# An mLSTM memory layer with its key transposes and one head's output transpose taken from TensorE to VectorE and DRAM

## The chip, the cores and the metric

One core of a Trainium2 chip runs the whole program. The metric is the device time of one execution in microseconds (us); the kernel before takes 935.12 us, the median of 3 runs (934.95 to 935.29). One further execution was profiled, and all durations and starting times below come from it.

## The reference, cut to what matters

The program is one inference step of a two-layer decoder: 256 prompt tokens and 64 sample tokens (8 sequences of 8) share the weights. Layer 0 mixes tokens by chunked spatial gating, layer 1 by an mLSTM matrix memory with 8 heads (keys of 128, values of 256), and each layer ends in a gated feed-forward part. The change lies in layer 1, the memory layer:

```
def step(carry, inp):
    C, n, m = carry
    qc, kc, vc, ic, fc = inp
    ...
    sc = jnp.einsum('bhtd,bhsd->bhts', qc, kc) * w_intra
    num = w_inter[..., None] * jnp.einsum('bhtd,bhde->bhte', qc, C) \
        + jnp.einsum('bhts,bhse->bhte', sc, vc)
    ...
    h = num / jnp.maximum(jnp.abs(den), jnp.exp(-m_t))[..., None]
    ...
    kg = kc * g[..., None]
    decay = jnp.exp(bL + m - m_new)
    C_new = decay[..., None, None] * C + jnp.einsum('bhsd,bhse->bhde', kg, vc)
```

After it each head's `h` is normalised over its 256 values, multiplied by a gate of `o`, and goes through the output projection. So a head needs its keys in two orders: key dimension on the partitions for the scores `sc`, and token on the partitions for `kg` (the new state contracts over tokens). And its normalised rows come out with the token on the partitions, while the output projection wants the value dimension there.

## The kernel before, in words

Weights stream from memory in chunks of 128 x 1024 numbers (`raw`). Products are made of three matmuls of split numbers: ScalarE rounds a chunk to `wh` (`CAST wh`, L181), VectorE makes the rest `wl = raw - wh` (L182), and TensorE does `xh wh`, `xl wh`, `xh wl` for each of the 8 slices, 24 matmuls a block into a PSUM tile `pm`. Four `raw` buffers are filled by SyncE, which waits in its queue until a buffer is free; there are three pairs `wh`, `wl`, so a chunk can be split only when the chunk three before it has been used up. The split of the next chunk is issued ahead of the current block.

The memory layer goes through the heads in pairs (`first_of` for the even head, `second_of` for the odd one). For a head: block q and block k (projections; L934 to L948 add the convolution and give `qs`, once for q and once for k); for an even head the values of both heads (`pv`, `pvs`); then

- `scores`: `psc` = key-query products on TensorE; VectorE makes `Pf` (L1057) from it, `weigh` splits it into `Ph`, `Pl` and makes `Ps`;
- `k_nat`: TensorE turns the keys by three transposes into the PSUM tile `pk` (`turn`): two for the 256 prompt keys, one for the sample keys. ScalarE and VectorE then make `kz` (sample keys with their gates, two halves: ScalarE L1090, VectorE L1091) and `kgh`, `kgl` (gated prompt keys, split, two halves each: L1095, L1096);
- an o block (`o_b`, L1208, then `th_o`);
- `hand_over`: `inter` (8 small matmuls of the old state, `num<-C,Qz`) and `state_sample` (16 matmuls `pcs`, first with the first half of `kz`, then with the second), then VectorE adds `pcs` to the decayed state `C` (L1136);
- `close`, after the following block: 11 matmuls `num`, and `state_prompt`: 6 matmuls `pCp` of `kgh`, `kgl` and the values, which ScalarE copies out (`Cp`, L1203);
- `stats`: the normalised rows `hn` on ScalarE (L1178), which need `nb` on VectorE (L1176) and `sl` on GpSimd. In the heads named in `OFF`, VectorE then turns `hn` in 32x32 blocks (`tb`, L1181), SyncE writes the tile to DRAM (`turn`) and reads it back in four pieces with the blocks exchanged (`hT`, in `back`), and `finish` multiplies it by the gate (`y_b`, six pieces, L1196) and splits the result (`yhb` L1230, `ylb` L1231). In the other heads (0 and 7) `finish` lets TensorE turn `hn` by six transposes into PSUM (`phn`, L53 and L57), and `y_b` (L1228) reads that. `finish(0)` stands inside the second o block of head 1, between its 5th and 6th slice.

Instructions of an engine run in one queue in the order in which they are written, rearranged ahead of time by a scheduler under `behind(...)`, which puts work after a named instruction. PSUM has 3 tiles for `pm`, `pk` and `pvs` and 5 for all else (`psc`, `num`, `pcs`, `pCp`, `pv`, `phn`).

Of the kernel before, what the change touches and what calls it, by code (L numbers as in the profile page):

```python
# [10 lines left out]
F32 = mybir.dt.float32  # L11
F32R = mybir.dt.float32r
# [28 lines left out]
class Net:  # L41
# [745 lines left out]
    def layer_b(self):  # L787
# [5 lines left out]
        with ExitStack() as ctx:  # L793
# [225 lines left out]
            def turn(h):  # L1019
                s = S[h]  # L1020
                ks = s["k"][0]
                s["pk"] = pk = self.psm.tile([P, 512], F32, tag="pm", name="pk")
                for t in range(3):
                    self.tr(pk[:, t * P:(t + 1) * P], ks[:, t * P:(t + 1) * P] if t < 2 else s["ks"], self.ident)

            def scores(h):
# [46 lines left out]
                                               mk[:, NB:NB + 1], Pr.bitcast(F32).rearrange("p (g s) -> p g s", g=4),  # L1073
                                               op0=MULT, op1=ADD)

            def k_nat(h):
                s = S[h]
                if h:
                    turn(h)
                pk = s["pk"]  # L1080
# [5 lines left out]
                kz = hp.tile([P, 2, P], F32R, tag="kz", name="kz", bufs=1)  # L1086
                src = pk[:, 2 * P:3 * P]

                for i in range(2):
                    nc.scalar.activation(kz[:, i, :], src, AF.Copy, scale=gm[:, i, h:h + 1])  # L1090
                    s["kz"] = nc.vector.scalar_tensor_tensor(kz[:, i, :], src, gm[:, 2 + i, h:h + 1], kz[:, i, :].bitcast(F32), op0=MULT, op1=ADD)  # L1091
                for t in range(2):
                    g = colsT[:, t, 32 + h:33 + h]
                    src = pk[:, t * P:(t + 1) * P]
                    nc.scalar.activation(kgh[:, t, :], src, AF.Copy, scale=g)  # L1095
                    nc.vector.scalar_tensor_tensor(kgl[:, t, :], src, g, kgh[:, t, :].bitcast(F32), op0=MULT, op1=SUB)  # L1096
                s["kg"] = (kgh, kgl, kz)
# [32 lines left out]
            def state_out(h, g):  # L1130
                s = S[h]
                dec, C0, pcs = s["P"][2], s["C"][g], s["pcs"][g]
                for u in range(2):
                    b = 2 * g + u
                    s["decayed"] = nc.scalar.activation(C0[:, u, :DV], C0[:, u, :DV], AF.Copy, scale=dec[:, b:b + 1])
                nc.vector.tensor_tensor(C0[:, :, :DV], C0[:, :, :DV], pcs.rearrange("p (u v) -> p u v", u=2), op=ADD)  # L1136
# [76 lines left out]
            def finish(h):  # L1213
                s = S[h]
                yh = hp.tile([P, 2, T], F32R, tag="yhb", name="yhb", bufs=6)
                yl = hp.tile([P, 2, T], F32R, tag="ylb", name="ylb", bufs=6)
                for e in range(2):
                    if h not in OFF:
                        pt = self.psa.tile([P, 512], F32, tag="pa", name="phn")
                        for t in range(2):  # L1220
                            self.tr(pt[:, t * P:(t + 1) * P], hn[:, t, e * P:(e + 1) * P], self.ident)
                        self.tr_some(pt[:, TP:384].rearrange("p (d g s) -> p d g s", d=2, g=4), hn[:, 2, e * P:(e + 1) * P],
                                     self.ident.rearrange("p (g d s) -> p d g s", g=4, d=2))
                    y = self.tp.tile([P, T], F32, tag="yf", name="y_b", bufs=2)
                    if h in OFF:
                        turned_y(h, e, y)
                    else:
                        nc.vector.scalar_tensor_tensor(y, s["o"][e], 1.0, pt[:, :T], op0=ADD, op1=MULT)  # L1228
                    g = gnh[:, 2 * h + e:2 * h + e + 1]
                    nc.scalar.activation(yh[:, e, :], y, AF.Copy, scale=g)  # L1230
# [25 lines left out]
            def blk():  # L1256
                return self.block(KD, self.x_rhs)
# [22 lines left out]

            def first_of(p):
                h = 2 * p
                ps = blk()
                close(h - 1)
                qk_epi(h, 0, ps)
                if h - 2 in OFF:
                    with self.behind(S[h - 1]["sent"]):
                        back(h - 2)
                ps = blk()
                qk_epi(h, 1, ps)  # L1290
                if h - 2 in OFF:
# [12 lines left out]
                v_out(p)  # L1304
                ps = blk()
                o_epi(h, 0, ps)
                hand_over(h)

            def second_of(p):
                h = 2 * p + 1  # L1310
                if p == 0:
                    with self.behind(chosen):
                        self.prefetch(0, self.used + 2)
                ps = blk()
                if p == 0:
# [12 lines left out]
                qk_epi(h, 1, ps)  # L1328
                if h - 2 in OFF:
                    with self.behind(S[h]["halves"][1]):  # L1330
                        finish(h - 2)
                state_in(h)
                ps = blk()
                o_epi(h - 1, 1, ps)
                stats(h - 1)
                if h < NH - 1:
                    rows_in(h + 1)
                if h < NH - 1:
                    ps = blk()
                    o_epi(h, 0, ps)  # L1340
                else:
                    for m in (4, 5):
                        out(m)
                scores(h)
                weigh(h)
                k_nat(h)
                if h == NH - 1:
                    for m in (6, 7):
                        out(m)
                if h == NH - 1:  # L1350
                    with self.behind(S[h - 1]["sent"]):
                        back(h - 1)
                    with self.behind(self.last_sum):
                        finish(h - 1)
                if h < NH - 1:
                    if p:
                        ps = blk()
                    else:
                        ps = self.psm.tile([P, 512], F32, tag="pm", name="pm")
                        (wh, wl), _ = self.take()  # L1360
                        self.rows(ps, wh, wl, 5, self.x_rhs, True, False)
                        finish(0)
                        self.rows(ps, wh[:, 5:, :], wl[:, 5:, :], 3, lambda k: self.x_rhs(5 + k), False, True)
# [4 lines left out]
                    hand_over(h)  # L1368

            scores(0)  # L1370
            k_nat(0)
            with self.behind(S[0]["kz"]):
                weigh(0)
            for p in range(NH // 2):
# [191 lines left out]
```

## Time and profile before

| | |
|---|---|
| median of the runs | 935.12 us |
| the profiled execution's own time | 935.03 us |
| its span from first to last instruction | 933.2 us |
| TensorE matmul (PE) busy | 926.8 us, 99% |
| VectorE (DVE) busy | 689.4 us, 74% |
| ScalarE (ACT) busy | 507.6 us, 54% |
| granted TensorE clock | 1.00 |
| the memory layer lies at about | 418 to 694 us |

A row of the timeline gives start, duration, engine, line, operation with its output and inputs, and in brackets how long the engine stood idle before it and what ended that. PE rows are matmuls, PEld rows the loading of their stationary operand; the ends of PE rows are modelled and overlap, so distances between starts of PEld rows tell more. Durations on the other engines include a part that overlaps the next instruction as well, so the distance of two starts (the pitch) is what an instruction takes in a full queue. In a row of the windows view each engine's busy time is followed by the number of its instructions, then come the granted clock, the share of DMA time and GB/s.

### The profile page before, as it was taken

The page shows a single profiled execution, that of the slowest core. Times are in us where ns is not written, and L with a number is a line of the kernel's source. Part 1 is how long each engine was busy: PE and PEld are TensorE (multiplying, and loading weights), DVE is VectorE, ACT ScalarE, POOL GpSimd, SP SyncE. Part 2 cuts the span into 40 slices and gives each one's busy share as a digit, 9 for nine tenths or more (in the row PEclk, how much of TensorE's full clock was granted, in tenths as well). Part 3 has the DMA queues.
Part 4 walks back from the last instruction along what each step waited for, and adds up shares of the span by engine and source line. Part 5 has one row for each costly group of instructions (what it writes and reads, how often), then busy time and mean ns, then how long its engine had stood idle before and what let it go on. Part 6 is the DMA issues. An engine that isn't in the chain of part 4 may idle for free.

```text
span 933.2 us, 16783 instructions
## 1 busy us (share of the span) xinstructions
PE 926.8 (99%) x6301; PEld 896.7 (96%) x6301; DVE 689.4 (74%) x1283; ACT 507.6 (54%) x892; POOL 110.9 (12%) x312
## 2 busy tenths in 40 slices
PE   9999999999999999999999999999999999999997
PEld 8889999999999999998989989989999999999997
DVE  6768985597777764458998999798788777775541
ACT  7558544455454543346777776575646454553341
POOL 2410000010000001013221112001003111100001
PEclk9999999999999999999999999999999999999999
DMA  8865444455455455457776878675475454455622
GB/s 290 239 192 170 136 139 157 144 151 153 144 156 146 148 155 146 145 166 231 212 239 202 256 228 252 196 240 172 149 222 155 143 156 145 149 152 152 202 68 69
DMA packets 64001, 162.62 MB, mean 174 GB/s; under 512 B 8608, under 2 KB 24744, under 8 KB 63920
## 3 DMA queue, kind: packets, MB, share of 16 engines
q1 hardware_dynamic: 63568, 160.56, 56.4%
q8 instruction: 50, 0.82, 0.4%
q0 software_dynamic: 208, 0.73, 0.2%
q14 instruction: 31, 0.25, 0.1%
q10 hardware_dynamic: 144, 0.26, 0.1%
HBM read 147.20 MB, written 14.32 MB: 173 GB/s over the span
## 4 chain that ended last, share of the span: by engine, by line
PE 96%; DVE 2%; DMA 0%; POOL 0%; issue 0%; ACT 0%; SPq 0%; DVEq 0%; ACTq 0%; POOLq 0%
PE pm L50 76%; PE pv L50 9%; PE pvs L50 3%; PE num L50 2%; PE pyt L50 1%; PE pmix L50 1%; PE py L50 1%; PE pCp L50 1%; PE pcs L50 1%; PE psc L50 0%; DMA raw<-in_a_wv 0%; DVE bcv L942 0%; DVE wl L182 0%; PE pk L53 0%; PE pyt L53 0%
## 5 line engine op out<-in xcount | busy, mean ns | idle before, releaser
L181 ACT CAST wh<-raw 128x1024 fp32r<-128x1024 f32 (+4 forms) x252 | 254.7, 1012 | 279.8 <-PE pm L50 143.4
L182 DVE TENSOR_TENSOR wl<-raw,wh 128x1024 fp32r<-128x1024 f32 (+4 forms) x252 | 299.1, 1187 | 111.9 <-ACT wh L181 109.4
L50 PE MATMUL pm<-xh,wh 128*128 128x320 f32 x1088 | 338.4, 311 | 0.0
L50 PE MATMUL pm<-xh,wl 128*128 128x320 f32 x1088 | 336.2, 309 | 0.0
L50 PE MATMUL pm<-xl,wh 128*128 128x320 f32 x1088 | 336.1, 309 | 0.0
L50 PEld LDWEIGHTS pm<-xh,wh 128*128 128x128 f32 x1088 | 204.3, 188 | 1.7 <-ACT wh L181 0.5
L50 PEld LDWEIGHTS pm<-xl,wh 128*128 128x128 f32 x1088 | 204.3, 188 | 0.2
L50 PEld LDWEIGHTS pm<-xh,wl 128*128 128x128 f32 x1088 | 204.2, 188 | 0.0
L50 PE MATMUL pm<-yh_f,wh 128*128 128x320 f32 x308 | 95.4, 310 | 0.0
L50 PE MATMUL pm<-yl_f,wh 128*128 128x320 f32 x308 | 95.1, 309 | 0.0
L50 PE MATMUL pm<-yh_f,wl 128*128 128x320 f32 x308 | 95.1, 309 | 0.0
L50 PEld LDWEIGHTS pm<-yl_f,wh 128*128 128x128 f32 x308 | 57.9, 188 | 0.0
L50 PEld LDWEIGHTS pm<-yh_f,wh 128*128 128x128 f32 x308 | 57.9, 188 | 0.0
L50 PEld LDWEIGHTS pm<-yh_f,wl 128*128 128x128 f32 x308 | 57.9, 188 | 0.0
L607 DVE SCALAR_TENSOR_TENSOR fcv<-fpad,vecs,fcv 128x336 f32<-128x336 f32 x88 | 49.7, 564 | 1.5
L50 PE MATMUL pv<-wh,xh 128*128 128x512 f32 (+1 forms) x132 | 50.3, 386 | 0.3 <-ACT wh L181 0.3
L50 PE MATMUL pv<-wl,xh 128*128 128x512 f32 (+1 forms) x132 | 50.1, 385 | 0.0
L50 PE MATMUL pv<-wh,xl 128*128 128x512 f32 (+1 forms) x132 | 50.0, 384 | 0.0
L347 DVE TENSOR_TENSOR xT<-pm,xT 128x320 f32<-128x320 f32 x38 | 18.5, 489 | 31.5 <-PE pm L50 31.5
L50 PE MATMUL pm<-yhb,wh 128*128 128x320 f32 x128 | 39.6, 310 | 0.0
L50 PE MATMUL pm<-yh_a,wh 128*128 128x320 f32 x128 | 39.6, 309 | 0.0
L50 PE MATMUL pm<-yl_a,wh 128*128 128x320 f32 x128 | 39.5, 309 | 0.0
(347 smaller groups left out, 1447.6 us busy)
## 6 DMA issues: line engine op xcount, KB each, us to landing
raw<-in_f_up SPq DMA_DIRECT2D x88, 512.0 KB, 3.6
raw<-in_b_win SPq DMA_DIRECT2D x32, 512.0 KB, 4.2
raw<-in_f_dn SPq DMA_DIRECT2D x28, 448.0 KB, 3.4
C<-in_C SPq DMA_DIRECT2D x32, 258.0 KB, 4.6
raw<-in_a_win SPq DMA_DIRECT2D x16, 512.0 KB, 3.7
raw<-in_a_wo SPq DMA_DIRECT2D x16, 512.0 KB, 3.6
raw<-in_b_wv SPq DMA_DIRECT2D x16, 512.0 KB, 3.5
out_Cs<-C SPq DMA_DIRECT2D x32, 256.0 KB, 3.4
```

The lines of the kernel that those rows point to most:

```text
L50: self.pin(self.nc.tensor.matmul(out, lhsT, rhs, start=start, stop=stop))
L181: self.last_split = nc.scalar.copy(wh[:, c, :], raw[:, c, :])
L182: self.last_low = nc.vector.tensor_tensor(wl[:, c, :], raw[:, c, :], wh[:, c, :].bitcast(F32), op=SUB)
L347: self.last_sum = self.nc.vector.tensor_tensor(x, ps[:, :T], x, op=ADD)
L607: nc.vector.scalar_tensor_tensor(cv, pd[:, i:i + NC], self.vec(w + i * KF), cv, op0=MULT, op1=ADD)
```

## The change

`OFF` gets head 0 as well: its `hn` is now turned by VectorE over DRAM, and `finish(0)` moves from the middle of head 1's second o block to the place in head 2 where the other heads have theirs. Its `y_b` is made by six VectorE instructions instead of two.

The prompt keys of heads 1 to 7 are no longer turned by TensorE: `turn` has one transpose left in these heads, the sample keys'. A new `k_turned`, called after block k, lets VectorE turn the 256 prompt keys in 32x32 blocks (`kb`, 128 x 256), writes them to DRAM (`kturn`), and reads them back in four pieces (`kn`, pieces of 64 numbers). `k_nat` is cut in two: `k_sample` makes `kz`, and `k_prompt` makes `kgh`, `kgl` from `kn`, later: behind the values' `vh`, `vl` in even heads, behind the state's decay and sum in odd heads, behind `finish(6)`'s `yh`, `yl` in head 7.

`state_prompt` of the odd heads moves from `close` to behind block k of the following head, so that its six matmuls stand directly in front of the values' `pv`.

```
-OFF = (1, 2, 3, 4, 5, 6)
+OFF = (0, 1, 2, 3, 4, 5, 6)
...
-                for t in range(3):
+                for t in range(2 if h else 0, 3):
                     self.tr(pk[:, t * P:(t + 1) * P], ...
...
+            def k_turned(h):
+                blocks = hp.tile([P, 4, 2, 32], F32, tag="kb", name="kb", bufs=1)
+                nc.vector.transpose(blocks.rearrange("p g t c -> p t g c"),
+                                    S[h]["k"][0][:, :TP].rearrange("p (t g q) -> p t g q", t=2, g=4))
+                nc.sync.dma_start(I["kturn"][h], blocks.rearrange("p g t c -> p (g t c)"))
+                S[h]["kn"] = kn = hp.tile([P, 4, 2, 32], F32, tag="kb", name="kn", bufs=1)
+                for g in range(4):
+                    nc.sync.dma_start(kn[32 * g:32 * g + 32].rearrange("p j t c -> p j (t c)"),
+                                      I["kturn"][h].rearrange("(j q) (g x) -> g q j x", j=4, g=4)[g])
...
-            def k_nat(h):
+            def k_sample(h):
...
+            def k_prompt(h):
...
+                    src = s["kn"][:, :, t, :] if h else s["pk"][:, t * P:(t + 1) * P].rearrange("p (j c) -> p j c", j=4)
+                    nc.scalar.activation(hi, src, AF.Copy, scale=g)
+                    nc.vector.scalar_tensor_tensor(lo, src, g, hi.bitcast(F32), op0=MULT, op1=SUB)
...
             def close(h):
...
-                if h < NH - 2:
+                if h % 2 == 0 and h < NH - 2:
                     state_prompt(h)
...
             def first_of(p):
...
                 ps = blk()
+                state_prompt(h - 1)
                 qk_epi(h, 1, ps)
+                k_turned(h)
...
-                k_nat(h)
+                k_sample(h)
                 values(p, 3)
                 v_out(p)
+                with self.behind(S[h]["vh"], S[h]["vl"]):
+                    k_prompt(h)
...
             def second_of(p):
...
                 qk_epi(h, 1, ps)
+                k_turned(h)
...
-                k_nat(h)
+                k_sample(h)
...
-                    if p:
-                        ps = blk()
-                    else:
...
-                        finish(0)
...
-                    o_epi(h, 1, ps)
+                    o_epi(h, 1, blk())
...
                     hand_over(h)
+                    with self.behind(S[h]["decayed"], S[h]["added"]):
+                        k_prompt(h)
```

The scheduler's order of VectorE in head 1, from the `Pf` of its scores to the second half of `kz`, which the second half of `pcs` needs. Before:

```order
L1057 SCALAR_TENSOR_TENSOR Pf<-psc,w 128x448
L182 TENSOR_TENSOR wl<-raw,wh 128x1024
L1042 SCALAR_TENSOR_TENSOR w<-mb,cols,mxb 128x64
L361 TENSOR_TENSOR Pl<-Pf,Ph 128x384
L1072 SCALAR_TENSOR_TENSOR Ps<-Pf,mk,Pr 128x4x16
L1091 SCALAR_TENSOR_TENSOR kz<-pk,gm,kz 128x128
L1228 SCALAR_TENSOR_TENSOR y_b<-th_o,phn 128x320 x2
L1091 SCALAR_TENSOR_TENSOR kz<-pk,gm,kz 128x128
```

The same stretch of VectorE's queue with the change:

```order
L1057 SCALAR_TENSOR_TENSOR Pf<-psc,w 128x448
L182 TENSOR_TENSOR wl<-raw,wh 128x1024
L1195 STREAM_TRANSPOSE tb<-hn 128x6x4x32
L361 TENSOR_TENSOR Pl<-Pf,Ph 128x384
L1072 SCALAR_TENSOR_TENSOR Ps<-Pf,mk,Pr 128x4x16
L1095 SCALAR_TENSOR_TENSOR kz<-pk,gm,kz 128x128
L1222 TENSOR_TENSOR o_b<-pm,rb 128x320
L1042 SCALAR_TENSOR_TENSOR w<-mb,cols,mxb 128x64
L182 TENSOR_TENSOR wl<-raw,wh 128x1024
L1095 SCALAR_TENSOR_TENSOR kz<-pk,gm,kz 128x128
```

The second `kz` has moved behind head 0's transpose, an `o_b` and the split of a further weight chunk; the two `y_b` that stood ahead of it are gone. Both of its halves still come from the PSUM tile `pk`.

The same stretch of VectorE's queue in head 3, before, from `Pf` on:

```order
L1057 SCALAR_TENSOR_TENSOR Pf<-psc,w 128x448
L1091 SCALAR_TENSOR_TENSOR kz<-pk,gm,kz 128x128
L182 TENSOR_TENSOR wl<-raw,wh 128x1024
L361 TENSOR_TENSOR Pl<-Pf,Ph 128x384
L1072 SCALAR_TENSOR_TENSOR Ps<-Pf,mk,Pr 128x4x16
L1091 SCALAR_TENSOR_TENSOR kz<-pk,gm,kz 128x128
L1208 TENSOR_TENSOR o_b<-pm,rb 128x320
L182 TENSOR_TENSOR wl<-raw,wh 128x1024
```

And with the change:

```order
L1057 SCALAR_TENSOR_TENSOR Pf<-psc,w 128x448
L1245 SCALAR_TENSOR_TENSOR ylb<-y_b,gnh,yhb 128x320 x2
L182 TENSOR_TENSOR wl<-raw,wh 128x1024
L1195 STREAM_TRANSPOSE tb<-hn 128x6x4x32
L361 TENSOR_TENSOR Pl<-Pf,Ph 128x384
L1072 SCALAR_TENSOR_TENSOR Ps<-Pf,mk,Pr 128x4x16
L1095 SCALAR_TENSOR_TENSOR kz<-pk,gm,kz 128x128
L1222 TENSOR_TENSOR o_b<-pm,rb 128x320
L182 TENSOR_TENSOR wl<-raw,wh 128x1024
L1095 SCALAR_TENSOR_TENSOR kz<-pk,gm,kz 128x128
```

Here `ylb` and `tb` stood in front of `Pf` before, so that these only changed sides; what is new in front of the second `kz` is the `o_b` and the second `wl`, which followed it before. The order in head 5 changes in the same way, but there four blocks of the output projection stand between the scores and `pcs`.

The last place is TensorE where the values of head 2 begin, with the change (`pv_5504` and `pv_5505` are the PSUM tiles of the two prompt halves; the words in brackets name the engine whose semaphore the matmul waits for):

```order
L50 MATMUL pCp_5443<-vl_4510,kgh_5330 128x258
L50 MATMUL pCp_5443<-vh_4509,kgl_5331 128x258
L50 MATMUL pv_5504<-wh_5415,xh_77 128x512 [waits DVE_49]
L50 MATMUL pv_5504<-wh_5415,xl_78 128x512
L50 MATMUL pv_5504<-wl_5416,xh_77 128x512
L50 MATMUL pv_5505<-wh_5415,xh_77 128x512 [waits Activation_49]
L50 MATMUL pv_5505<-wh_5415,xl_78 128x512
```

Before, block k with its 24 matmuls stood between the last `pCp` and the first `pv`. Three of the five PSUM tiles hold head 1's `num` until `hn` is made, the fourth is `pCp`, the fifth the first `pv`; the second `pv` gets the tile of `pCp`, once ScalarE has copied it out. In ScalarE's queue that copy (`Cp`) stood ahead of a `CAST wh` and of q's `CAST qh` before, and stands directly behind these two now; heads 4 and 6 have the same order on both engines.

More of the change, by code (lines that the diff above doesn't have):

```diff
@@ L1079, in k_nat @@
                     turn(h)
-                pk = s["pk"]
+                kz = hp.tile([P, 2, P], F32R, tag="kz", name="kz", bufs=1)
+                src = s["pk"][:, 2 * P:3 * P]
+                for i in range(2):
+                    nc.scalar.activation(kz[:, i, :], src, AF.Copy, scale=gm[:, i, h:h + 1])
+                    s["kz"] = nc.vector.scalar_tensor_tensor(kz[:, i, :], src, gm[:, 2 + i, h:h + 1], kz[:, i, :].bitcast(F32), op0=MULT, op1=ADD)
+                s["kg"] = (None, None, kz)
+            def k_prompt(h):
+                s = S[h]
                 if h < NH - 2:
@@ L1085, in k_nat @@
                     kgh, kgl = self.late_keys(h)
[L1086 to L1091, printed above, removed]
                 for t in range(2):
                     g = colsT[:, t, 32 + h:33 + h]
[L1094 to L1097, printed above, removed]
+                    src = s["kn"][:, :, t, :] if h else s["pk"][:, t * P:(t + 1) * P].rearrange("p (j c) -> p j c", j=4)
+                    hi, lo = [x[:, t, :].rearrange("p (j c) -> p j c", j=4) for x in (kgh, kgl)]
+                    nc.scalar.activation(hi, src, AF.Copy, scale=g)
+                    nc.vector.scalar_tensor_tensor(lo, src, g, hi.bitcast(F32), op0=MULT, op1=SUB)
+                s["kg"] = (kgh, kgl, s["kg"][2])
             def rows_in(h):
@@ L1135, in state_out @@
                     s["decayed"] = nc.scalar.activation(C0[:, u, :DV], C0[:, u, :DV], AF.Copy, scale=dec[:, b:b + 1])
-                nc.vector.tensor_tensor(C0[:, :, :DV], C0[:, :, :DV], pcs.rearrange("p (u v) -> p u v", u=2), op=ADD)
+                s["added"] = nc.vector.tensor_tensor(C0[:, :, :DV], C0[:, :, :DV], pcs.rearrange("p (u v) -> p u v", u=2), op=ADD)
                 s["sent"] = nc.sync.dma_start(O["Cs"][h, :, 2 * g:2 * g + 2, :], C0[:, :, :DV])
@@ L1354, in second_of @@
                         finish(h - 1)
+                    with self.behind(S[h - 1]["yh"], S[h - 1]["yl"]):
+                        k_prompt(h)
                 if h < NH - 1:
-                    if p:
-                        ps = blk()
-                    else:
-                        ps = self.psm.tile([P, 512], F32, tag="pm", name="pm")
-                        (wh, wl), _ = self.take()
-                        self.rows(ps, wh, wl, 5, self.x_rhs, True, False)
-                        finish(0)
-                        self.rows(ps, wh[:, 5:, :], wl[:, 5:, :], 3, lambda k: self.x_rhs(5 + k), False, True)
-                    o_epi(h, 1, ps)
+                    o_epi(h, 1, blk())
                     if p == 2:
@@ L1548 @@
     O = {k: nc.dram_tensor("out_" + k, s, F32, kind="ExternalOutput").ap() for k, s in _OUTS.items()}
-    for k, v in dict(rows=(8, 456), sums=(1, 11 * P), turn=(NH, P, 3 * DV)).items():
+    for k, v in dict(rows=(8, 456), sums=(1, 11 * P), turn=(NH, P, 3 * DV), kturn=(NH, P, TP)).items():
         I[k] = nc.dram_tensor(k, v, F32, kind="Internal").ap()
```

6 lines of the change are left out of this document (4 added, 2 removed).

## Prediction

> **What bounds the kernel now.** I read the page's totals first, then the chain of waits, the windows of the memory layer, the waits of PEld, and last the timelines of the engines around the places that the change touches.
>
> ```profile
> PE 926.8 (99%) x6301; PEld 896.7 (96%) x6301; DVE 689.4 (74%) x1283; ACT 507.6 (54%) x892; POOL 110.9 (12%) x312
> PE 96%; DVE 2%; DMA 0%; POOL 0%; issue 0%; ACT 0%; SPq 0%; DVEq 0%; ACTq 0%; POOLq 0%
> 446.00:473.00 27.00, 26.90 (x226) 24.63 (x228) 25.49 (x66) 20.94 (x53) 7.93 (x19) 1.00 0.72 226
> 473.00:525.00 52.00, 52.00 (x370) 48.00 (x370) 47.85 (x109) 37.78 (x83) 8.60 (x19) 1.00 0.73 230
> 525.00:578.00 53.00, 53.00 (x376) 48.84 (x367) 50.25 (x119) 39.18 (x86) 8.39 (x23) 1.00 0.80 243
> PEld pcs L50 <- DVE kz L1091: 0.8, 2, 0.4
> PEld pw L50 <- issue: 0.8, 1, 0.8
> ```
>
> TensorE sets the time: 99% busy, 96% of the chain. So a matmul taken away is worth its time, and a new wait of TensorE costs its whole length. VectorE's 74% is a mean; in the three windows of heads 1 to 5 it is busy 25.49 of 27, 47.85 of 52 and 50.25 of 53 us, 92 to 95%. Moving work from TensorE to VectorE here puts it on an engine that has 5 to 8% left, and TensorE does wait for it already: for `kz`, in front of `pcs`.
>
> **What TensorE loses.** The loads in head 1, at the key transposes and at the first head's output transposes:
>
> ```profile
> 466.68 0.26 PEld L53 LDWEIGHTS pk<-ident,qs 128*128 128x128 f32 x2
> 466.91 0.14 PEld L53 LDWEIGHTS pk<-ident,ks 128*128 128x128 f32 x1
> 467.02 0.19 PEld L50 LDWEIGHTS pm<-xh,wh 128*128 128x128 f32 x1
> ...
> 469.18 0.30 PEld L53 LDWEIGHTS phn<-ident,hn 128*128 128x128 f32 x2
> 469.80 0.14 PEld L57 LDWEIGHTS phn<-ident,hn 128*128 128x128 f32 x1 [0.32 <-ACT hn L1178]
> ...
> 470.19 0.19 PEld L50 LDWEIGHTS pm<-xh,wh 128*128 128x128 f32 x1
> ```
>
> Three key transposes take 467.02 - 466.68 = 0.34 us, 0.115 each. Two go in each of seven heads: 14 x 0.115 = 1.6 us. Head 0's six `phn` take 470.19 - 469.18 = 1.0 us, with the 0.32 that they wait for `hn`. Together 2.6 us off the bound engine; were everything else free, the profiled execution of 935.03 would come to 932.4. All else in this sum is a wait.
>
> [...]
>
> **What VectorE gets, and the second half of kz in head 1.** VectorE in head 1, and the group of the existing block transposes:
>
> ```profile
> 465.31 0.27 DVE L361 TENSOR_TENSOR khl<-qs,kh 128x128 fp32r<-128x128 f32 x1
> ...
> 468.08 0.16 DVE L1176 SCALAR_TENSOR_TENSOR nb<-mv,sl 128x3 f32<-128x3 f32 x1 [0.75 <-POOL sl L1167]
> ...
> 468.56 0.61 DVE L1057 SCALAR_TENSOR_TENSOR Pf<-psc,w 128x448 f32<-128x448 f32 x1
> 469.10 1.21 DVE L182 TENSOR_TENSOR wl<-raw,wh 128x1024 fp32r<-128x1024 f32 x1
> ...
> 471.21 0.34 DVE L1091 SCALAR_TENSOR_TENSOR kz<-pk,gm,kz 128x128 fp32r<-128x128 f32 x1
> 471.48 0.87 DVE L1228 SCALAR_TENSOR_TENSOR y_b<-th_o,phn 128x320 f32<-128x320 f32 x2
> 472.27 0.34 DVE L1091 SCALAR_TENSOR_TENSOR kz<-pk,gm,kz 128x128 fp32r<-128x128 f32 x1
> ```
>
> ```profile
> L1181 DVE STREAM_TRANSPOSE tb<-hn 128x768 f32<-128x768 f32 x6 | 5.8, 968 | 1.3 <-ACT hn L1178 1.3
> ```
>
> A new `kb` has 256 of `tb`'s 768 columns: 968 x 256/768 = 0.32 us, an estimate. From the queue's order in head 1, what lands ahead of the second `kz` is `kb` 0.32, `tb` 0.9 (0.97 less its overlap), an `o_b` 0.40 and a weight split 1.13 (pitches from the rows of head 3 below); the two `y_b` in front of it go, 472.27 - 471.48 = 0.79. Sum: 1.96 us. It ends at 472.27 + 0.34 + 1.96 = 474.57. Who waits:
>
> ```profile
> 472.72 0.19 PEld L50 LDWEIGHTS pcs<-vh,kz 32*128 32x128 f32 x4 [0.41 <-DVE kz L1091]
> ...
> 472.95 0.20 PEld L50 LDWEIGHTS pcs<-vh,kz 32*128 32x128 f32 x4
> ```
>
> The second half of `pcs` loads at 472.95. With the transposes gone TensorE is 0.23 + 1.0 us earlier, ready at 471.7; it gets `kz` at 474.6 (0.05 from VectorE's end to the load, as in head 3). A wait of 2.9 us. Behind it in TensorE's queue stands all that follows, first the next o block. VectorE's queue is full here but for 0.75 us in which `nb` waits for `sl`; that pause doesn't absorb `kb`, since GpSimd's `sl` starts from VectorE's `rd`, which stands behind `kb` and is delayed with it. Bounds for this wait: 1.7 us, if the split ahead of `kz` costs nothing, and 3.3, if ScalarE's second `kz`, now behind a `CAST`, comes later still.
>
> **The same in head 3.**
>
> ```profile
> 519.31 0.32 DVE L361 TENSOR_TENSOR khl<-qs,kh 128x128 fp32r<-128x128 f32 x1 [0.16 <-ACT kh L360]
> ...
> 525.44 0.34 DVE L1091 SCALAR_TENSOR_TENSOR kz<-pk,gm,kz 128x128 fp32r<-128x128 f32 x1
> 525.70 0.47 DVE L1208 TENSOR_TENSOR o_b<-pm,rb 128x320 f32<-128x320 f32 x1
> 526.10 1.21 DVE L182 TENSOR_TENSOR wl<-raw,wh 128x1024 fp32r<-128x1024 f32 x1
> 527.23 0.34 DVE L1096 SCALAR_TENSOR_TENSOR kgl<-pk,cols,kgh 128x128 fp32r<-128x128 f32 x1
> ```
>
> ```profile
> 525.83 0.19 PEld L50 LDWEIGHTS pcs<-vh,kz 32*128 32x128 f32 x4
> ```
>
> `kz` ends at 525.78 and `pcs` loads at 525.83: no slack today. Ahead of it come `o_b` (526.10 - 525.70 = 0.40), the split (527.23 - 526.10 = 1.13) and `kb`, 0.32 less the 0.16 for which `khl` waits now: 1.69 us. `pcs` then loads at 527.52; TensorE, 0.23 earlier, is ready at 525.60. A wait of 1.9 us; bounds 0.8, without the split, and 2.4. The wait in head 1 doesn't pay for this one, since VectorE is tied to TensorE again between the two:
>
> ```profile
> 512.77 1.05 ACT L181 CAST wh<-raw 128x1024 fp32r<-128x1024 f32 x1 [0.50 <-PE pm L50]
> ```
>
> ```profile
> 513.86 1.23 DVE L182 TENSOR_TENSOR wl<-raw,wh 128x1024 fp32r<-128x1024 f32 x1 [0.29 <-ACT wh L181]
> ```
>
> A split waits for its cast, the cast for TensorE to be done with a chunk; a later TensorE means a later queue. In head 5 four output blocks stand ahead of `pcs`, in head 7 as well, and in even heads both halves stand ahead of the values' work: no wait, 0.23 us gained in each, counted above.
>
> **The copy of pCp.** In heads 2, 4 and 6 the second `pv` now waits for ScalarE's copy. Head 6, where block k ends at 602.21, with ScalarE and the copy's group:
>
> ```profile
> 602.21 0.39 PE L50 MATMUL pv<-wh,xh 128*128 128x512 f32 x1
> ...
> 602.90 0.39 PE L50 MATMUL pv<-wh,xh 128*128 128x512 f32 x1
> ```
>
> ```profile
> 602.30 1.05 ACT L181 CAST wh<-raw 128x1024 fp32r<-128x1024 f32 x1 [0.55 <-PE pm L50]
> 603.26 0.40 ACT L360 CAST qh<-qs 128x256 fp32r<-128x256 f32 x1
> 603.57 0.67 ACT L940 ACTIVATE bcv<-bpad,vecs 128x344 f32<-128x344 f32 x1
> ```
>
> ```profile
> L1203 ACT COPY Cp<-pCp 128x258 f32<-128x258 f32 x6 | 2.2, 374 | 1.3 <-PE pCp L50 1.3
> ```
>
> Counted from the end of block k: the cast can't start before it (it waits for that block's buffers), `qh` is through 1.36 us after it, the copy 0.37 later, at 1.73. TensorE meanwhile does six `pCp` (three key transposes took 0.34; six such, 0.7) and three `pv` (602.90 - 602.21 = 0.69), and is ready at 1.39. A wait of 0.4 us with its release; in heads 2 and 4, where VectorE lags and the cast stands behind a `bth` that ends later, I take 0.5. Together 1.4; bounds 0, if the copy comes in time, and 2.7, with 0.9 each.
>
> **Transfers.** Each of seven heads adds a write and four reads to SyncE's queue, head 0 the same for `hT`; SyncE waits there for `kb`, then for the write, with raw loads behind it.
>
> ```profile
> turn<-tb SPq DMA_DIRECT2D x6, 384.0 KB, 2.3
> hT<-turn SPq DMA_DIRECT2D x24, 96.0 KB, 3.8
> SPq L162 <- DVE wl L182: 574.5, 205, 7.6
> ```
>
> By these rows `kn` is there 6 to 7 us after `kb`; head 1's `kb` goes in where `khl` starts now, 465.31, and ends near 465.6; its `kgh` comes behind `pcs`, after 474: covered by 2 us. SyncE spends 574.5 us waiting for free `raw` buffers, so some us more for `kturn` let a load start later and still early. I cost both at nothing; if the cover goes, it is a rival below.
>
> **Sum.** -2.6 + 2.9 + 1.9 + 1.4 = +3.6: 935.03 becomes 938.6 us. The profiled execution lies 0.09 below the median, so the same number stands against it. With the bounds, -2.6 + 1.7 + 0.8 + 0 = -0.1 to -2.6 + 3.3 + 2.4 + 2.7 = +5.8: 934.9 to 940.8.
>
> **The rivals.** (a) VectorE's queue absorbs it, the other side: the second `kz` comes before TensorE needs it, at 471.7 in head 1 and 525.6 in head 3, and the copy in time. From VectorE being 2.9 and 1.9 us ahead of where I have it, only the 2.6 stay: 932.4. For it speaks that VectorE has 74% over the whole span; against it the 95% of the window and the `kz` wait that exists. Chance 0.15.
> (b) Only one of the two `kz` waits is there and the copy costs nothing: -2.6 + 1.9 or + 2.9, 934.3 to 935.3. For it: the split moved up also leaves the later queue emptier. Chance 0.13.
> (c) TensorE's clock: it is granted 1.00 in all windows, and TensorE never stops for longer than the 0.8 us of the row for `pw`; 2.9 us hasn't been seen. If the clock halves after such a stop for as long as the stop lasted, that costs half of it, 1.4 and 0.9 us: up to 941.0. [...] Chance 0.04.
> (d) `kn` late: if the round trip takes over 9 us in place of 6 to 7, ScalarE stops at `kgh` and with it the casts behind it; 1 us in each of three odd heads gives 941.6. Chance 0.04.
> That the change doesn't do what it says is out: the new order has one key transpose per head left.
>
> **Numbers.** The forecast has 0.64 at 938.6. A measurement of this kernel can tell about 0.2% from no change, 1.9 us. Faster by more (below 933.2) is (a), 0.15; same (933.2 to 937.0) is (b), cut to 0.13 as its top lies inside; slower has the rest, 0.72, the forecast's own lower end being unlikely. The range leaves out (a) and the top of (c) and (d), about 0.2 together: 934.2 to 940.6.
>
> **What would show it.** In the changed kernel's waits PEld `pcs` should wait for `kz` some 5 us in two places, 2.9 in head 1 and 1.9 in head 3; PEld `pv` for ScalarE's `Cp` three times, 0.4 to 0.5 each; the `pk` loads should be a third. I am wrong if the `kz` waits stay at 0.8 us in all, or if TensorE waits for `kgh`, `wl` or `wh` instead. A granted clock under 1.00 after head 1 would speak for (c).

## The result and the profile after

The changed kernel takes 940.52 us (median of 6 executions, 938.30 to 942.91) against 935.32 us before on the same chips (6 executions, 934.95 to 935.88): a ratio of 1.0056, 95% interval 1.0041 to 1.0072, or 5.2 us slower. The profiled execution took 940.69 us, with a span of 939.0 us.

The executions of the changed kernel lie 4.6 us apart, those of the kernel before 0.9 us, and the changed kernel's times go with the clock that TensorE was granted over each execution:

| granted clock | 0.999 | 0.997 | 0.997 | 0.997 | 0.995 | 0.993 |
|---|---|---|---|---|---|---|
| us | 938.30 | 940.02 | 940.34 | 940.69 | 941.40 | 942.91 |

The page's totals and the chain of waits after the change, and the windows of heads 1 to 5:

```profile
PE 928.0 (99%) x6281; PEld 896.5 (95%) x6281; DVE 691.1 (74%) x1295; ACT 507.6 (54%) x892; POOL 110.3 (12%) x312
PE 90%; DVE 4%; DMA 2%; ACT 1%; issue 1%; POOL 0%; SPq 0%; DVEq 0%; ACTq 0%
446.00:473.00 27.00, 26.20 (x214) 24.10 (x212) 25.01 (x64) 20.53 (x50) 7.73 (x18) 1.00 0.72 215
473.00:525.00 52.00, 50.06 (x333) 45.89 (x334) 45.96 (x113) 34.59 (x75) 7.79 (x21) 0.97 0.77 237
525.00:578.00 53.00, 51.10 (x357) 46.08 (x357) 48.64 (x112) 37.64 (x83) 7.90 (x21) 1.00 0.80 243
```

TensorE's part of the chain falls from 96 to 90%, VectorE's doubles from 2 to 4%, and DMA and ScalarE rise from 0 to 2 and 1%. In the two windows in which TensorE was busy throughout it now stands still for 1.9 us each. VectorE isn't busier there than before (45.96 us instead of 47.85, 48.64 instead of 50.25): it was not short of time in the mean, its work came in another order. And in the middle row the granted clock, the number behind the five engines, is 0.97 instead of 1.00.

What PEld waits for, the new rows:

```profile
PEld pcs L50 <- DVE kz L1095: 3.0, 2, 1.6
PEld pcs L50 <- PE num L50: 2.9, 3, 1.6
PEld pv L50 <- ACT Cp L1217: 2.1, 3, 0.7
```

The second row is misleading: `pcs` stands behind `num` in TensorE's own queue, but `num` had long been done; the first half of `kz` came last. So `pcs` waits some 5 to 6 us for `kz`, where it was 0.8, and `pv` three times for the copy.

Head 1, first TensorE's loads, then VectorE from the first to the second half of `kz`:

```profile
473.28 0.22 PEld L50 LDWEIGHTS pcs<-vh,kz 32*128 32x128 f32 x4 [1.57 <-PE num L50]
473.39 0.22 PEld L50 LDWEIGHTS pcs<-vl,kz 32*128 32x128 f32 x4
475.21 0.19 PEld L50 LDWEIGHTS pcs<-vh,kz 32*128 32x128 f32 x4 [1.60 <-DVE kz L1095]
```

```profile
471.23 0.97 DVE L1195 STREAM_TRANSPOSE tb<-hn 128x768 f32<-128x768 f32 x1
...
472.83 0.34 DVE L1095 SCALAR_TENSOR_TENSOR kz<-pk,gm,kz 128x128 fp32r<-128x128 f32 x1
473.09 0.47 DVE L1222 TENSOR_TENSOR o_b<-pm,rb 128x320 f32<-128x320 f32 x1
473.49 0.27 DVE L1042 SCALAR_TENSOR_TENSOR w<-mb,cols,mxb 128x64 f32<-128x64 f32 x1
473.68 1.22 DVE L182 TENSOR_TENSOR wl<-raw,wh 128x1024 fp32r<-128x1024 f32 x1
474.82 0.34 DVE L1095 SCALAR_TENSOR_TENSOR kz<-pk,gm,kz 128x128 fp32r<-128x128 f32 x1
```

TensorE waits 1.57 us for the first half, works through eight small matmuls, and waits 1.60 us for the second, which ends at 475.16, behind `tb`, `o_b`, `w` and the split. In head 3 it is the same with shorter stops, 0.88 and 1.40 us:

```profile
529.77 0.22 PEld L50 LDWEIGHTS pcs<-vh,kz 32*128 32x128 f32 x4 [0.88 <-PE num L50]
...
531.50 0.19 PEld L50 LDWEIGHTS pcs<-vh,kz 32*128 32x128 f32 x4 [1.40 <-DVE kz L1095]
```

Then comes what the sum did not have. The windows of half a microsecond after head 1's stop (busy times of PE, PEld, DVE, ACT, POOL; the number behind them is the granted clock):

```profile
474.50:475.00 0.50, 0.00 (x0) 0.00 (x0) 0.50 (x2) 0.50 (x3) 0.00 (x0) 1.00 1.19 291
475.50:476.00 0.50, 0.50 (x10) 0.36 (x7) 0.18 (x1) 0.50 (x2) 0.00 (x0) 1.00 0.93 369
476.00:476.50 0.50, 0.50 (x5) 0.50 (x4) 0.50 (x2) 0.50 (x3) 0.00 (x0) 0.93 1.11 361
476.50:477.00 0.50, 0.50 (x4) 0.50 (x3) 0.50 (x2) 0.50 (x2) 0.00 (x0) 0.50 0.88 238
...
479.00:479.50 0.50, 0.50 (x4) 0.50 (x3) 0.00 (x0) 0.00 (x0) 0.00 (x0) 0.50 1.02 352
479.50:480.00 0.50, 0.50 (x4) 0.50 (x4) 0.00 (x0) 0.00 (x0) 0.00 (x0) 0.65 1.08 358
480.00:480.50 0.50, 0.50 (x5) 0.50 (x4) 0.00 (x0) 0.00 (x0) 0.00 (x0) 1.00 0.97 336
```

From 476.4 to 479.85, 3.4 us, TensorE runs at half its clock. It had been at work again for over a microsecond when that began. Up to TensorE's last matmul no window of the kernel before, nor any other window of this execution in steps of 10 us, shows a clock under 0.995.

The six times of the changed kernel fit such stretches. An estimate from these numbers: one stretch of 3.4 us at half clock takes 3.4 / 2 / 939 = 0.0018 off the clock of an execution, so 0.997, 0.995 and 0.993 would be one, two and three of them against 0.999, and the times rise by 0.7 to 2.4 us from one to the next, 4.6 us over three. Only the execution of 940.69 us was profiled; its trace has one.

The loads of the two kernels can be set side by side: the same instruction's start after the change less its start before, and where that difference jumps.

| place | jump, us |
|---|---|
| start of the memory layer (`pb`), ahead of all that changed | +0.4 |
| one transpose of `pk` left of three, in each of 7 heads | -0.23 each, -1.6 |
| head 0's `phn` | -1.0 |
| head 1, first and second half of `pcs` | +1.15 and +1.70 |
| head 1's following block, halved clock | +1.5 |
| `pv` in heads 2, 4, 6, net of what its first tile gives back | +0.50, +0.56, +0.50 |
| head 3, first and second half of `pcs` | +0.46 and +1.32 |

With 0.2 us from the program's opening these make +5.7 us; the spans differ by 5.8. All other differences are under 0.15 us.

### The profile page after: what moved, and what is told of

Read it like the earlier page. It is cut to its first block, busy times and chain, and to the rows that moved or that the text cites. A ratio compares the mean times of both kernels' runs of the same rounds, so it can differ in the third digit from the quotient of the medians.

```text
span 939.0 us, 16820 instructions
## 1 busy us (share of the span) xinstructions
PE 928.0 (99%) x6281; PEld 896.5 (95%) x6281; DVE 691.1 (74%) x1295; ACT 507.6 (54%) x892; POOL 110.3 (12%) x312
## 4 chain that ended last, share of the span: by engine, by line
PE 90%; DVE 4%; DMA 2%; ACT 1%; issue 1%; POOL 0%; SPq 0%; DVEq 0%; ACTq 0%
PE pm L50 72%; PE pv L50 9%; PE pvs L50 3%; PE pyt L50 1%; DVE wl L182 1%; PE num L50 1%; PE pmix L50 1%; DMA hT<-turn 1%; PE py L50 1%; ACT wh L181 1%; DVE bcv L942 1%; DMA bst<-in_b_state 1%; DMA raw<-in_a_wv 0%; DVE C L1150 0%; PE pcs L50 0%
## 5 line engine op out<-in xcount | busy, mean ns | idle before, releaser
L50 PE MATMUL pm<-yh_a,wl 128*128 128x320 f32 x128 | 39.5, 309 | 0.0
```

The lines of the kernel that those rows point to most:

```text
L50: self.pin(self.nc.tensor.matmul(out, lhsT, rhs, start=start, stop=stop))
```

## Experiments

The theory, after the trace: (1) the changed order puts VectorE's work ahead of the second `kz` in heads 1 and 3; (2) `pv` waits for the copy of `pCp`; (3) a long stop of TensorE is followed, in most executions, by half the clock for 3.4 us. The rival: what costs time is the new work itself, the round trips over DRAM and VectorE's transposes, and the clock varies for reasons of its own. Each trial ran against the kernel before on the same chip (935.2 to 935.4 us). The first and the last trial edit the kernel before, all others the changed kernel. Where the table of jumps is used again, it is made in the same way from the trial's profiled execution.

**Head 0's part alone**

```
-OFF = (1, 2, 3, 4, 5, 6)
+OFF = (0, 1, 2, 3, 4, 5, 6)
...
-                    if p:
-                        ps = blk()
-                    else:
...
-                        finish(0)
...
+                    ps = blk()
```

Expected:

> Only head 0's part of the change: its normalised rows are turned by VectorE over DRAM; the keys stay with TensorE and pCp stays where it was. Theory (the changed order puts VectorE work ahead of the second kz; TensorE waits; the clock halves after the long stop in head 1): in this kernel no weight split stands ahead of kz in head 1, only tb 0.9 and o_b 0.4 in place of y_b 0.8, so TensorE gains 1.0 and waits about 1.2 us more in head 1: 935 to 936, clock 1.00, head 3 as before. Rival (the DRAM round trips and VectorE's extra load as such cost the time): slower in proportion to its share of the new work, 936.5 or more.

Measured: 935.17 us, ratio 0.9997 (0.9989 to 1.0006). The jumps are -1.00 at `phn` and +0.49 and +0.62 at head 1's `pcs`: what TensorE saves it waits for, and nothing else moved. This part costs nothing and brings nothing, as expected.

**The keys' part alone**

The changed kernel with `OFF` and `finish(0)` as before.

> Only the keys' part, with all seven round trips; head 0 as before. Theory: the order keeps kz early in head 1 (a wait longer by about 0.4 us), has o_b and a split ahead of it in head 3 (1.9 us), and the copy of pCp costs 0.5 in three heads: -1.6 + 0.4 + 1.9 + 1.5 = +2.2, about 937.5, clock 1.00 in every run since no stop is near 3 us. Rival (round trips): nearly all of the loss, 939.5 to 940.5.

Measured: 940.00 us, ratio 1.0045 (1.0031 to 1.0058), so the number was the rival's, not mine. The trace says why. The sizes in head 3 are as foreseen (+0.46 and +1.32), but in head 2 `pv` waits longer for the copy than in the whole change (2.0 us, a jump of +1.87 instead of +0.50), and behind head 3's stop the clock was halved, which costs 1.5 us:

```profile
PEld pv L50 <- ACT Cp L1217: 3.4, 3, 2.0
PEld pcs L50 <- DVE kz L1095: 2.2, 3, 1.4
```

```profile
525.00:530.00 5.00, 3.38 (x43) 2.31 (x41) 4.80 (x9) 5.00 (x13) 0.00 (x0) 1.00 0.66 206
530.00:535.00 5.00, 5.00 (x31) 4.90 (x24) 3.01 (x6) 2.84 (x9) 0.69 (x3) 0.66 0.91 308
```

My expectation had taken 3 us as what a stop needs; here some 2.3 us in two pieces did it, while the 2.0 us in one piece in head 2 did not. By itself this trial could not tell the theories apart.

**All splits held back behind kz**

```
+                    with self.behind(S[h]["kz"]):
+                        self.prefetch(0, self.used + 2)
                     o_epi(h, 1, blk())
```

> The whole change, but in heads 1, 3 and 5 the next two weight splits are put behind the second kz. All transposes and round trips stay. Theory: the waits in heads 1 and 3 fall from 3.2 and 1.8 us to under 0.7 together, the clock stays 1.00: 940.5 - 2.5 - 1.5 - 1.7 = 934.8, within 0.8. Rival (round trips, VectorE's load): no change from the changed kernel, 939.5 to 941.

Measured: 941.02 us, ratio 1.0060 (1.0047 to 1.0073): a miss. The waits for `kz` did fall, in head 1 to +0.37 and in head 3 to +0.42, but the edit also held back the split that the very next block needs, and in head 5 that block is an output block that starts early:

```profile
PEld pm L50 <- DVE wl L182: 3.7, 3, 2.9
PEld pv L50 <- ACT Cp L1217: 3.2, 3, 1.8
```

One stop of 2.9 us went and another of 2.9 us came, with the clock halved behind it again (a jump of +1.5 us over the following block, 0.997 over the whole execution). It shows that the clock doesn't answer to `kz` or head 1 as such: a stop of another kind in another head is followed by the same half clock.

**Throwaway matmuls in head 1**

```
                 for i in range(2):
+                    if h == 1:
+                        for _ in range(13):
+                            mm(s["pcs"][0][:, DV:2 * DV], vh[:, 0, 1, :P], vh[:, 0, 1, :DV], True, True)
                     for v in (vh, vl):
```

> The whole change, and in head 1 two times 13 throwaway matmuls (128x256) ahead of the first and the second half of pcs, into a part of the PSUM tile that is overwritten: TensorE works where it stood still, kz is as late as before. Theory (the clock halves because TensorE stood still, for some 3.4 us, which costs 1.5 us in most executions and more in some): clock 1.00 in all runs, 938.3 to 939.2, and the runs lie within 1 us of each other instead of within 4.6. Rival (the clock loss has nothing to do with the stop): as the changed kernel, 940.5, clock 0.993 to 0.999, or slower by what the added matmuls take.

Measured: 941.19 us, ratio 1.0061 (1.0048 to 1.0073). The profiled execution (940.00 us) shows no halved clock, and the five times fall in two groups by their clock: 939.93 and 940.00 at 0.999, 941.19, 941.67 and 942.27 at 0.997. The 26 matmuls filled the stop and a little more (`pcs` +1.76 and +1.96 in place of +1.15 and +1.70). That is outside the expected 938.3 to 939.2, and inconclusive alone: head 3's stop was still there.

**Throwaway matmuls in heads 1 and 3, fewer**

The same edit with 10 and 10 in head 1, 4 and 9 in head 3.

> The whole change, with throwaway matmuls of 128x256 ahead of pcs in head 1 (10 and 10) and now in head 3 too (4 and 9), fewer than fill the stops. Theory (the clock halves for some 3.4 us after TensorE has stood still; in the last trial the runs with a granted clock of 0.997 were 1.2 to 2.3 us slower than those with 0.999, because head 3's stop was still there): clock 0.999 or 1.00 in all runs, all of them between 938.0 and 939.6. Rival (the clock varies from run to run for other reasons): a run or two at 0.997 and above 940.5, as with head 1 alone.

Measured: 940.11 us, ratio 1.0051 (1.0039 to 1.0063); the five executions have a clock of 0.999 or 1.00 and lie between 939.32 and 940.23. Heads 1 and 3 in their windows:

```profile
470.00:475.00 5.00, 5.00 (x51) 3.94 (x51) 5.00 (x10) 5.00 (x14) 0.69 (x3) 1.00 0.69 212
475.00:480.00 5.00, 5.00 (x42) 4.73 (x41) 3.51 (x9) 3.68 (x10) 0.00 (x0) 1.00 0.68 235
...
530.00:535.00 5.00, 5.00 (x41) 4.72 (x41) 3.68 (x10) 3.81 (x11) 0.69 (x3) 1.00 1.03 325
```

The spread went from 4.6 to 0.9 us and no execution lost clock, with `kz` as late as before. That is the theory's part (3). The level is 0.5 us above the top of what I expected, and only 0.4 us below the changed kernel's. Of the excess 0.36 us is longer stops (+1.40 and +1.60 in head 1, +0.68 and +1.31 in head 3), as the added matmuls run into them; the rest I can't place.

**pCp back in close, nothing else**

```
-                if h % 2 == 0 and h < NH - 2:
+                if h < NH - 2:
                     state_prompt(h)
...
-                state_prompt(h - 1)
                 qk_epi(h, 1, ps)
```

> The whole change, but the six pCp matmuls of the odd heads stand in close again, ahead of block k, as before the change. Theory: the three waits of pv for ScalarE's copy (0.50, 0.56 and 0.50 us net in the trace) go and nothing else: 940.5 - 1.6 = 938.9, with the kz waits of 3.2 and 1.8 us unchanged and the clock at 0.997 to 0.999. Rival (the copy's wait only moves the loss, since kgh and kgl come late over DRAM): num or pCp waits for kgh instead, 940.5.

Measured: 940.56 us, ratio 1.0056 (1.0045 to 1.0068), no gain: a miss by 1.7 us. `pv` no longer waits for the copy, and neither `num` nor `pCp` waits for `kgh`, so the rival's reason isn't there either. But this execution's clock was halved for 6.83 us behind head 1, from 473.45 to 480.28 (a jump of 2.6 us instead of 1.5), and once more for 3.41 us behind head 3 (0.993 over the whole execution):

```profile
470.00:475.00 5.00, 2.54 (x35) 1.29 (x33) 4.22 (x9) 5.00 (x14) 0.69 (x3) 0.85 0.78 244
475.00:480.00 5.00, 5.00 (x23) 4.99 (x20) 3.01 (x6) 2.25 (x7) 0.00 (x0) 0.50 0.87 290
480.00:485.00 5.00, 5.00 (x38) 5.00 (x38) 3.76 (x10) 2.23 (x5) 0.34 (x2) 0.97 0.28 81
```

And its end is longer, behind TensorE's last matmul: ScalarE's queue takes 2.83 us to issue the last output, which took 0.37 before. The kernel before, then this one:

```profile
929.20 0.37 ACTq L752 DMA_DIRECT2D out_y<-yo  x1
```

```profile
935.34 2.83 ACTq L752 DMA_DIRECT2D out_y<-yo  x1
```

That adds about 2 us to this execution, at a place that the edit doesn't touch; the cause is open. A term of 1.6 us can't be read from such a kernel; it had to be measured where nothing else stops TensorE.

**Two splits behind kz, the next chunk's not held**

```
             def first_of(p):
                 h = 2 * p
+                with self.behind(S[h - 1]["kz"]):
+                    self.prefetch(0, self.used + 2)
                 ps = blk()
```

> The whole change, with only the splits of the second and third chunk put behind the second kz in heads 1 and 3 (the chunk that is needed next stays ahead, unlike in the trial that held all splits back). pCp stays in front of pv. Theory: kz is 2.3 us earlier: wait about 0.6 us net in head 1, none in head 3, no halved clock; pv still waits for the copy, 1.6 to 2.7 us net in three heads: -2.6 + 0.6 + 2.1 = 935.4, within 0.8. Rival (round trips): 939 or more.

Measured: 938.88 us, ratio 1.0041 (1.0029 to 1.0053): a miss, 3.5 us above what I expected and at the rival's 939. The jumps are +0.67 and +0.53 in head 1 (double what I expected), +0.42 in head 3, and `pv` +1.38, +0.54 and +0.49; up to TensorE's last matmul no clock is lost in the trace. That matmul starts 1.7 us later than in the kernel before, not 0.1 as the theory had it; the remaining 2 us are the slow last issue once more (2.79 us in this trace). So the trial shows where the waits are, and its total is no clean measure.

**All three side effects undone**

The edit above, `pCp` in `close`, and `tb` of the head before held behind the second `kz`:

```
-                if h in OFF:
+                if h in OFF and (h % 2 or h == NH - 2):
+                    turn_rows(h)
+
+            def turn_rows(h):
+                if h in OFF:
                     turned = hp.tile([P, 4, 6, 32], F32, tag="tb", name="tb", bufs=1)
...
                     o_epi(h, 1, blk())
+                    with self.behind(S[h]["kz"], self.last_low):
+                        turn_rows(h - 1)
```

> All transposes and round trips of the change, with its three side effects undone: in heads 1, 3 and 5 the block transpose tb of the head before and the splits of the second and third weight chunk come behind the second kz, and the pCp of odd heads stand in close. Theory: only the matmuls taken away stay, -1.6 - 1.0: 932.5 to 933.3, clock 1.00, pcs waiting for kz 0.8 us in all or less. Rival (the round trips and VectorE's added work cost time as such): 935 or more.

Measured: 933.84 us, ratio 0.9986 (0.9977 to 0.9995): faster than both kernels, by 1.4 us than the kernel before and 6.7 us than the changed one, with every transpose and every round trip of the change in it. It lies 0.5 us above my range and 1.2 us below the rival's. The rival falls. Its totals, and head 1:

```profile
PE 925.2 (99%) x6281; PEld 895.7 (96%) x6281; DVE 691.2 (74%) x1295; ACT 508.2 (55%) x892; POOL 111.5 (12%) x312
```

```profile
472.06 0.22 PEld L50 LDWEIGHTS pcs<-vh,kz 32*128 32x128 f32 x4 [0.92 <-PE num L50]
...
472.78 0.19 PEld L50 LDWEIGHTS pcs<-vh,kz 32*128 32x128 f32 x4 [0.39 <-DVE kz L1095]
```

`kz` is still 1.0 us late in head 1 and 0.4 in head 3, and that is what is missing to the 2.6 us of matmuls taken away: -2.6 + 1.0 + 0.4 = -1.2 in the trace.

**The same with pCp in front of pv again**

> The version with the three side effects undone (933.84 us), with one of them put back: the six pCp of the odd heads again directly in front of pv. kz stays early. Theory (pv's second tile waits for ScalarE's copy, net 0.5 us in heads 4 and 6 and 0.5 to 1.5 in head 2): 935.3 to 936.3, clock 1.00 as no stop exceeds 1.5 us. Rival (the copy's wait was only part of the loss from the long stops, as the trial that moved pCp alone showed no gain): 933.5 to 934.3.

Measured: 936.51 us, ratio 1.0012 (1.0003 to 1.0021), 2.7 us above the version with `pCp` in `close`; 0.2 above my range, and far from the rival's. No clock is lost. The copy's wait is a term of its own, and it is largest in head 2:

```profile
PEld pv L50 <- ACT Cp L1221: 2.8, 3, 1.5
```

The jumps are +1.29, +0.55 and +0.50. In the changed kernel and the two trials with throwaway matmuls, where head 1's `pcs` loses 2.85 us or more, head 2 shows only 0.50; where it loses 1.2 us or less, the trials show 1.29 to 1.87: the late `kz` makes TensorE come later there and hides part of this wait.

**A late kz in the kernel before**

```
+                spent = []
...
-                    s["kz"] = nc.vector.scalar_tensor_tensor(kz[:, i, :], src, ...)
+                    with self.behind(*spent):
+                        s["kz"] = nc.vector.scalar_tensor_tensor(kz[:, i, :], src, ...)
+                    if h == 1 and i == 0:
+                        spare = hp.tile([P, 4, 6, 32], F32, tag="tb", name="spare", bufs=1)
+                        last = s["kz"]
+                        for _ in range(3):
+                            with self.behind(last):
+                                last = nc.vector.transpose(spare..., hn...)
+                        spent = [last]
```

> The kernel before, with three unused block transposes of 128x768 on VectorE ahead of the second kz of head 1 alone: no round trip, no moved work, one late kz. They take 2.7 to 2.9 us. Theory: TensorE stops about 2.5 to 2.9 us longer there, 938.0 at a granted clock of 0.999 to 1.00, and runs with a clock of 0.997 come out another 1.5 us higher, up to 939.7; at least two of five runs are of that kind. Rival (the halved clock of the changed kernel has to do with its transfers or with what follows in its order): all runs at 938.0 with the clock at 0.999 or 1.00.

Measured: 938.52 us, ratio 1.0037 (1.0024 to 1.0049), in two groups: 937.17, 937.35 and 937.43 at a clock of 0.999 or 1.00, and 939.62, 940.42 and 941.02 at 0.998 to 0.995. The first group lies 0.6 to 0.8 us under the expected 938.0, the second reaches 1.3 us above the expected 939.7. The profiled execution, 940.42 us, is of the second kind. In it `pcs` is 1.4 and 1.0 us later, and behind that stop stand:

```profile
476.50:477.00 0.50, 0.50 (x9) 0.33 (x6) 0.50 (x2) 0.50 (x2) 0.00 (x0) 0.59 0.00 0
477.00:477.50 0.50, 0.50 (x3) 0.50 (x4) 0.50 (x3) 0.50 (x3) 0.00 (x0) 0.50 0.13 33
...
480.00:480.50 0.50, 0.50 (x5) 0.50 (x4) 0.43 (x1) 0.00 (x0) 0.00 (x0) 0.99 0.28 88
```

The half clock is a jump of 1.5 us again; a further 0.97 us of this execution lie ahead of head 1, at the program's opening and the start of the memory layer. Here there are no new transfers and no moved `pCp`, only one late operand, and the halved clock is in the trace; the times of two more executions point to it. So a stop of TensorE is enough to bring it.

## Why the prediction was right, and what it missed

The measured 940.52 us lies in the range, 0.08 us below its upper end, and the direction is right: the measured +5.2 us stands against a forecast of +3.6. That the median still fell inside is luck: three of the six executions lie above 940.6, and what lifted them, the half clock, is not in the sum. The waits, which are, came out as forecast.

- **What TensorE loses**: 14 key transposes and six `phn`, -2.6 us. The jumps are -0.23 in each head and -1.0. Right.
- **The second half of kz in head 1**: 2.9 us forecast, 1.15 + 1.70 = 2.85 measured. The path was as worked out: `kb` (a pitch of 465.91 - 465.55 = 0.36 us instead of my 0.32), `tb`, `o_b`, split. What I had as one wait for the second half is two, since the first half of `kz` stands behind `tb` as well. Putting `tb` and the splits behind `kz`, with all work left in, takes it down to 1.0.

```profile
465.55 0.43 DVE L1078 STREAM_TRANSPOSE kb<-qs 128x256 f32<-128x256 f32 x1
465.91 0.28 DVE L361 TENSOR_TENSOR khl<-qs,kh 128x128 fp32r<-128x128 f32 x1
```

- **The same in head 3**: 1.9 forecast, 1.78 measured. That head 1's wait would not pay for it held too. Here also the forecast's one wait is two, 0.46 and 1.32, since the first half of `kz` no longer stands directly behind `Pf`.
- **The copy of pCp**: 1.4 forecast, 0.50 + 0.56 + 0.50 = 1.56 measured. My reason for head 2 (ScalarE behind there) was better than my number; with `kz` 1.0 us late instead of 2.85 that wait is 1.29 us.

```profile
487.45 0.19 PEld L50 LDWEIGHTS pv<-wh,xh 128*128 128x128 f32 x1 [0.67 <-ACT Cp L1217]
542.25 0.19 PEld L50 LDWEIGHTS pv<-wh,xh 128*128 128x128 f32 x1 [0.72 <-ACT Cp L1217]
609.13 0.19 PEld L50 LDWEIGHTS pv<-wh,xh 128*128 128x128 f32 x1 [0.67 <-ACT Cp L1217]
```

- **Transfers**: costed at nothing, and no cost of theirs shows: TensorE never waits for `kgh`, and the version with the side effects undone has them all. The new write lands after 3.1 us and the reads after 2.3 (medians), 5.4 in place of the 6 to 7 that I took from `turn` and `hT`:

```profile
kturn<-kb SPq DMA_DIRECT2D x7, 128.0 KB, 3.1
kn<-kturn SPq DMA_DIRECT2D x28, 32.0 KB, 2.3
```

- **The sum**: the four measured terms make -2.6 + 2.85 + 1.78 + 1.56 = +3.6, the forecast's number. The fastest execution, whose clock stayed at 0.999, took 938.30 us against the 938.6 predicted.

The step that failed is rival (c), TensorE's clock, which I gave 0.04 and left out of the sum. I had let it halve, if at all, for as long as the stop lasted, and no trace stood behind the 0.04: the longest wait of TensorE in the profile before is 0.8 us. In the traces it is halved for 3.41 us, which costs 1.5 us, or for twice that (6.83 us, 2.6 us of time, with `pCp` back in `close`), and the stop doesn't have to be whole: in head 1 it is two pieces of 1.6 us with matmuls between them, in the keys' trial 0.9 and 1.4 us in head 3. So it should have stood in the sum as the common case; the sign that I had named for it, a clock under 1.00 after head 1, is there.

Which stop is followed by half the clock can't be told from its length alone. The waits of PEld in the profiled executions, and the clock behind them:

| place | waits of PEld, us | clock behind them |
|---|---|---|
| head 2, the keys' part alone | 2.0 | 1.00 |
| head 3, changed kernel | 0.88 and 1.40 | 1.00 |
| head 3, throwaway matmuls in head 1 | 0.88 and 1.40 | 1.00 |
| head 3, the keys' part alone | 0.88 and 1.40 | 0.66 in the mean of 5 us |
| head 3, `pCp` back in `close` | 0.88 and 1.40 | 0.50 for 3.41 us |
| head 1, late `kz` in the kernel before | 0.41, 1.08 and 0.82 | 0.50 for 3.41 us |
| head 5, all splits held back | 2.87 | halved; 0.997 over the whole execution |
| head 1, changed kernel | 1.57 and 1.60 | 0.50 for 3.41 us |
| head 1, `pCp` back in `close` | 1.5 and 1.6 | 0.50 for 6.83 us |

The same two waits in head 3 were followed by half the clock in two of the four profiled executions that have them. TensorE need not have stood still throughout: in the changed kernel the 3.41 us ahead of the fall at 476.43 hold matmuls from 473.3 to 473.8 and from 475.2 on, and 1.68 us of standing still. Up to TensorE's last matmul every fall of the clock in the profiled executions is in this table. What exactly halves the clock stays open.

Rivals (a), (b) and (d) fell: VectorE's queue absorbed nothing, both `kz` waits were there, and `kgh` was never waited for by TensorE.

About 0.4 us at the start of the memory layer in the profiled execution lies ahead of all that was changed; in the profiled executions of the trials the same place shows between 0 and +0.5, so I count it as chance.

## What to carry to other kernels

Where one engine sets the time and another is 92 to 95% busy, moving work to the second is decided by its queue: look for the operand that the first engine waits for already and count what the new order puts in front of it; here 2.6 us of saved matmuls cost 6.2 us of waits, and an order that kept that operand and the copy of `pCp` in front brought 1.4 us with the same work. Before moving a producer next to the consumer of its PSUM tile's successor, find the copy that frees the tile in its engine's queue; here its wait cost 1.56 us in three heads. And add to a stop of TensorE the half clock that can follow it, 1.5 us or more: here it followed waits of 2.3 to 3.2 us in sum, whole or in pieces, and whether the same stop brought it differed from one execution to the next.

## What the runs showed of the hardware

- A granted clock of 0.50 for 3.41 us or twice that. In the changed kernel it starts 1.2 us after TensorE had resumed for good (475.21 and 476.43). Whether it comes differs from execution to execution, and the times of such kernels spread over 1.7 to 4.6 us, those of the others over 0.9 to 1.9. With throwaway matmuls in the stops of heads 1 and 3 the clock stayed at 0.999 to 1.00 in five executions.
- VectorE's transpose of 128x256 takes 0.44 us in the mean, the one of 128x768 0.97 us; TensorE's transpose of 128x128 takes 0.115 us of a full queue.
- In the profiled executions of two kernels the last output took 2.8 us to issue from ScalarE's queue instead of 0.37, which made the end of the program 2 us longer. Why is open; nothing in those edits touches that place.
